# Three gate projections by one level of Strassen's algorithm, moved behind the attention stages

## The chip, the cores and the metric

The kernel runs on one core of a Trainium2 chip. The metric is the device time of one execution in microseconds (us); the time before is the median of three runs.

## The reference, cut to what matters

One encoder layer for 512 tokens of width 1024, all in float32. What the change touches are the three gates, the three branch outputs and their merge:

```python
u = rmsnorm(h, g_mix)                       # (512, 1024)
proj = u @ w_in                             # columns: GLA q,k,v,gg,alpha | FoX q,k,v,f | mq | 3 gates x 1024
y_gla = (rmsnorm(gla(...), g_gla_head) * silu(gg)) @ w_gla_o     # (512,512) @ (512,1024)
y_fox = forgetting_attention(...) @ w_fox_o
y_mem = memory_attention(...) @ w_mem_o
gt = sigmoid(gates.reshape(B, S, 3, D))     # gates = u @ the last 3 x 1024 columns of w_in
merged = gt[:, :, 0] * y_gla + gt[:, :, 1] * y_fox + gt[:, :, 2] * y_mem
h = h + merged @ w_out
u2 = rmsnorm(h, g_ffn)
h = h + square(relu(u2 @ w_ff1)) @ w_ff2
return rmsnorm(h, g_final)
```

## The kernel before, in words

Every large product is done as three matmuls (`mm3`, L151 to L153): both operands are split into a high part (a cast to the reduced format fp32r, on ScalarE, ACT) and a low part (the rest, by a subtraction on VectorE, DVE), and high by high, high by low and low by high are summed in PSUM. Weights come from HBM in chunks of 128 x 1024 (512 KB, by SyncE's queue, SP, into a ring of three `raw` tiles); `get_w` loads one and splits it into `hi` and `lo` tiles, rings of three each (L142, L143 for most; `split`, L201 and L202, elsewhere).

Two helpers use a chunk. `gT` keeps 128 output columns of the weight stationary and streams all 512 tokens (u is held transposed, channels on partitions, as `uhi` and `ulo`): 8 steps of 3 matmuls, and the result is transposed, channels by tokens. `gN` keeps 128 tokens stationary and streams 512 weight columns: the result has tokens on partitions. Both are generators: a *unit* is one step of three matmuls with 512 moving columns, and `weave` puts a given number of units of filler behind each step of an attention stage, so that TensorE (PE) has work while ACT and DVE do the softmax or the decays. The order of instructions on PE is the order written in the code. On the other engines a scheduler sets it when the program is built, and each engine, and the DMA queue of each, then works in that order.

The stages in order: the projections of memory and of u (front); FoX attention in 4 pairs of heads (`fox_scores`, `fox_turn`, `fox_values`), filled with projections; memory attention in 4 heads (`mem_scores`, `mem_turn`, `mem_values`), filled with `branch("gate_fox", ...)`; GLA (`decays`, `key_turn`, `gla_scores`, `states`, `gla_intra`, `gla_values`, `gla_turn`), filled with `branch("gate_mem", ...)`; then `branch("gate_gla", ...)` alone; then the product with `w_out`, the norm, and the MLP, both of whose products are already done by one level of Strassen's algorithm (7 block products in place of 8).

`branch` goes over 8 tiles of 128 channels: 24 matmuls for the gate, tanh on ACT (a sigmoid up to scale), 12 matmuls for the branch output, DVE multiplies both (L607), GpSimd (POOL) adds to `acc` (L608). The third branch also splits the sum into `mh` and `ml` (L611, L612), the stationary operands of `w_out`.

In the MLP's second product, `factor` makes sums of weight blocks by a DMA that adds in SBUF: SP loads a block into `b11` or `b12`, and POOL's queue (L1044) adds the next one onto it after the block before has been split. Sums of blocks of `w_ff1` (`T1` to `T4` for each quarter, 32 transfers in all) are made in HBM by POOL's queue beforehand (`next_sum`, L127 and L129), each released by the cast of some weight chunk.

Names in the order of instructions: `mm` and `a` are PSUM tiles (four banks each), `hi`/`lo`/`whi`/`wlo`/`flo` split weights, `th` the gate's tanh.

Of the kernel before, what the change touches and what calls it, by code (L numbers as in the profile page):

```python
# [9 lines left out]
F32 = mybir.dt.float32  # L10
# [7 lines left out]
P = 128  # L18
# [14 lines left out]
def chunk_list():  # L33
# [29 lines left out]
def hybrid_block(ctx, tc, chunks, wst, xT, memT, xN, cols, gffn, gfin, wup, cst, out):  # L63
# [140 lines left out]
    def sq_cols(pool_, src, n, k, accs, pool_ks, tag):  # L204
# [3 lines left out]
        if accs[e] is None:  # L208
            accs[e] = pool_.tile([P, n], F32, tag=f"{tag}_acc{e}", name=nm("acc"))
# [47 lines left out]
    sg = [gp.tile([P, S], F32, name=f"sg{j}") for j in range(4)]  # L257
    ofh = [ofp.tile([P, S], F32R, name=f"ofh{j}") for j in range(4)]
# [6 lines left out]
    with pool("front") as fp:  # L265
        rmb = gv[:, 0, 0:M]
        rxb = fp.tile([P, S], F32, name="rxb")
# [88 lines left out]
        for k in range(KT):  # L356
            ut = fp.tile([P, S], F32, tag="ut", name=nm("ut"), bufs=3)
# [216 lines left out]
    edge = mst.enter_context(pool("edge", side="right"))
    edge.tile([P, 112], F32, name="edge_pad")
    mp = mst.enter_context(pool("merge", side="right"))
    acc = [mp.tile([P, S], F32, name=f"acc{j}") for j in range(KT)]

    ogp = mst.enter_context(pool("ogla", side="right"))
    ogh = [ogp.tile([P, S], F32R, name=f"ogh{j}") for j in range(4)]  # L580
    ogl = [ogp.tile([P, S], F32R, name=f"ogl{j}") for j in range(4)]
    omst = ExitStack()
    omp = omst.enter_context(pool("omem", side="right"))
    omh = [omp.tile([P, S], F32R, name=f"omh{j}") for j in range(4)]
    oml = [omp.tile([P, S], F32R, name=f"oml{j}") for j in range(4)]

    def branch(gate, wo, oh, ol, n, last=None):
        cur = {}

        def gate_evac(ps):  # L590
            cur["th"] = th = mp.tile([P, S], F32, tag="th", name=nm("th"))
            nc.scalar.activation(th, ps, AF.Tanh, scale=0.5)

        for j in range(KT):
            yield from gT(("T", "w_in", OFF[gate] + P * j), uhi, ulo, gate_evac)
            th = cur["th"]
            if j % 2 == 0:
                ow = [t.rearrange("p (j k c) -> p j k c", j=2, k=4) for t in get_w(("O", wo, j // 2))]
            py = mmt()
            for k in range(4):  # L600
                mm3(py, ow[0][:, j % 2, k, :], ow[1][:, j % 2, k, :], oh[k], ol[k], k == 0, k == 3)
                if k < 3:
                    yield
            if n == 0:
                nc.vector.scalar_tensor_tensor(acc[j], th, 1.0, py, op0=ALU.add, op1=ALU.mult)
            else:
                nc.vector.scalar_tensor_tensor(th, th, 1.0, py, op0=ALU.add, op1=ALU.mult)  # L607
                nc.gpsimd.tensor_tensor(acc[j], acc[j], th, op=ALU.add)  # L608
            if last is not None:
                h, l = last  # L610
                nc.scalar.mul(h[:, j, :], acc[j], 0.5)  # L611
                nc.vector.scalar_tensor_tensor(l[:, j, :], acc[j], 0.5, f(h[:, j, :]), op0=ALU.mult, op1=ALU.subtract)  # L612
            yield


    with pool("mematt") as ap:
# [3 lines left out]
        def mem_q(h):  # L620
# [3 lines left out]
            return proj(OFF["mq"] + P * h, evac)  # L624
# [34 lines left out]
        def mem_values(h):  # L659
# [5 lines left out]
            split(omh[h], oml[h], po)  # L665
# [9 lines left out]
    ofst.close()  # L675


    with pool("gla") as lp:
        NC = 8
        half = [slice(64 * e, 64 * e + 64) for e in range(2)]  # L680
        gs = {}

        def decays(j):
            pb = at_()
            for t in range(NT):
                nc.tensor.matmul(pb[:, t * P:(t + 1) * P], la[:, t, j * P:(j + 1) * P], tri64, start=True, stop=True)
            ep, en, ek, kn, kp = (lp.tile([P, S], F32, name=f"{n}{j}") for n in ("ep", "en", "ek", "kn", "kp"))
            bl = small(lp, NC, f"bl{j}").rearrange("p (c o) -> p c o", o=1)
            dec = small(lp, NC, f"dec{j}")
            ek3, pb3 = (x.rearrange("p (c t) -> p c t", c=NC) for x in (ek, pb))  # L690
            nc.vector.tensor_copy(bl, pb3[:, :, 63:64])
            nc.vector.tensor_tensor(ek3, pb3, bl.to_broadcast([P, NC, 64]), op=ALU.subtract)
            nc.scalar.activation(ep, pb, AF.Exp)
            nc.scalar.activation(en, pb, AF.Exp, scale=-1.0)
            nc.scalar.activation(ek, ek, AF.Exp, scale=-1.0)
# [544 lines left out]
```

## Time and profile before

| | |
|---|---|
| runs | 831.17, 831.18, 829.07 us; median 831.17 us |
| profiled execution | 831.07 us, of which the traced span is 829.3 us |
| granted TensorE clock, mean | 0.992 |
| busy, share of the span | PE 98%, PE weight load 84%, DVE 63%, ACT 50%, POOL 14% |
| moved | 148.15 MB, mean 179 GB/s |

The profile has times in microseconds from the start of the span and one line for an instruction or a group of them (the line in the code, the engine, the operation, the tile written, an arrow, the tiles read, the shape, a count). Matmuls overlap, so that what one costs is the distance between two starts, not its listed duration. The three stages of attention lie at 91 to 208 us (FoX), 208 to 310 us (memory) and 310 to 381 us (GLA); the third branch ends at 454.5 us, the norm behind `w_out` at about 513 us, the MLP at about 820 us.

### The profile page before, as it was taken

To read this page: it belongs to the slowest core of one execution; us is meant where nothing else is said; L and a number is where in the kernel's file an instruction comes from. 1 tells how busy PE (TensorE), PEld (TensorE's weight loads), DVE (VectorE), ACT (ScalarE), POOL (GpSimd) and SP (SyncE) were. 2 spreads that over 40 slices of the span, in tenths; PEclk is the share of its full clock that TensorE was granted. 3 is DMA by queue.
4 is the path that set the end of the run, shared out by engine and by line. 5 is a ranking of instruction groups with operands and counts; after the bars stand their busy time and mean duration, and the time that the engine had idled before them with its cause. 6 is when DMAs were issued, how large, how long until landed. Compare 5 with 4: busy or idle time off the path is not lost.

```text
span 829.3 us, 11999 instructions
## 1 busy us (share of the span) xinstructions
PE 812.4 (98%) x4665; PEld 693.0 (84%) x4665; DVE 521.5 (63%) x799; ACT 417.5 (50%) x672; POOL 116.4 (14%) x124
## 2 busy tenths in 40 slices
PE   8999999999999999999999999999999999999994
PEld 5888787787888888888888889988998899889983
DVE  5783535554344546556434458895788778878886
ACT  7673544453233434233323336775676367547764
POOL 5211211000000001242122100011001100100122
PEclk9999999999999999999999999999999999999998
DMA  8445654335554637359676624878758966895674
GB/s 312 146 153 179 174 163 142 107 128 143 162 137 163 183 133 197 120 181 308 182 224 178 204 77 136 273 166 222 234 169 198 217 215 166 193 261 192 142 139 127
DMA packets 37577, 148.15 MB, mean 179 GB/s; under 512 B 4568, under 2 KB 5648, under 8 KB 35472
## 3 DMA queue, kind: packets, MB, share of 16 engines
q1 hardware_dynamic: 27648, 94.93, 32.7%
q0 software_dynamic: 8032, 47.71, 27.1%
q10 hardware_dynamic: 1840, 4.75, 1.7%
q8 instruction: 36, 0.59, 0.3%
q14 instruction: 21, 0.17, 0.1%
HBM read 143.68 MB, written 31.49 MB: 211 GB/s over the span
## 4 chain that ended last, share of the span: by engine, by line
PE 95%; DVE 2%; DMA 1%; issue 1%; ACT 0%; SPq 0%; POOLq 0%; POOL 0%; DVEq 0%
PE mm L151 27%; PE mm L153 26%; PE mm L152 26%; PE a L152 3%; PE a L151 3%; PE a L153 3%; PE a L479 1%; PE a L517 1%; DMA cst_s<-in_cst_dram 1%; DMA memr<-in_memT_dram 1%; PE a L503 0%; PE a L656 0%; PE a L855 0%; DVE h L908 0%; PE a L506 0%
## 5 line engine op out<-in xcount | busy, mean ns | idle before, releaser
L143 DVE TENSOR_TENSOR wlo<-raw,whi 128x1024 fp32r<-128x1024 f32 x75 | 97.3, 1300 | 112.7 <-ACT whi L142 111.9
L142 ACT CAST whi<-raw 128x1024 fp32r<-128x1024 f32 x75 | 78.6, 1051 | 138.9 <-PE mm L152 100.7
L151 PE MATMUL mm<-uhi,whi 128*128 128x512 f32 x352 | 139.4, 396 | 0.0
L152 PE MATMUL mm<-ulo,whi 128*128 128x512 f32 x352 | 137.3, 390 | 0.0
L153 PE MATMUL mm<-uhi,wlo 128*128 128x512 f32 x352 | 137.1, 389 | 0.0
L201 ACT CAST hi<-raw 128x1024 fp32r<-128x1024 f32 x65 | 68.2, 1050 | 47.5 <-PE mm L152 34.4
L202 DVE TENSOR_TENSOR lo<-raw,hi 128x1024 fp32r<-128x1024 f32 x65 | 79.5, 1223 | 18.6 <-ACT hi L201 18.6
L151 PEld LDWEIGHTS mm<-uhi,whi 128*128 128x128 f32 x352 | 66.1, 188 | 15.2 <-issue 1.8
L153 PEld LDWEIGHTS mm<-uhi,wlo 128*128 128x128 f32 x352 | 66.1, 188 | 14.1
L152 PEld LDWEIGHTS mm<-ulo,whi 128*128 128x128 f32 x352 | 66.2, 188 | 12.9
L1044 POOL DMA_DIRECT2D b<-in_wst_dram x32 | 27.6, 864 | 264.1 <-DVE lo L202 203.0
L153 PE MATMUL mm<-u2h,lo 128*128 128x256 f32 x224 | 63.4, 283 | 0.0
L152 PE MATMUL mm<-u2l,hi 128*128 128x256 f32 x224 | 63.4, 283 | 0.0
L151 PE MATMUL mm<-u2h,hi 128*128 128x256 f32 x224 | 63.4, 283 | 0.0
L151 PE MATMUL mm<-hi,ch 128*128 128x512 f32 x160 | 62.2, 389 | 0.0
L152 PE MATMUL mm<-lo,ch 128*128 128x512 f32 x160 | 62.2, 389 | 0.0
L153 PE MATMUL mm<-hi,cl 128*128 128x512 f32 x160 | 62.2, 389 | 0.0
L201 ACT CAST hi<-b 128x1024 fp32r<-128x1024 f32 x40 | 41.9, 1049 | 38.0 <-PE mm L153 27.2
L202 DVE TENSOR_TENSOR lo<-b,hi 128x1024 fp32r<-128x1024 f32 x40 | 48.9, 1223 | 18.0 <-ACT hi L201 17.7
L151 PE MATMUL mm<-u2sh,hi 128*128 128x256 f32 x168 | 47.5, 283 | 0.0
L152 PE MATMUL mm<-u2sl,hi 128*128 128x256 f32 x168 | 47.5, 283 | 0.0
L153 PE MATMUL mm<-u2sh,lo 128*128 128x256 f32 x168 | 47.5, 283 | 0.0
(334 smaller groups left out, 1810.6 us busy)
## 6 DMA issues: line engine op xcount, KB each, us to landing
raw<-in_wst_dram SPq DMA_DIRECT2D x121, 512.0 KB, 4.8
b<-in_wst_dram POOLq DMA_DIRECT2D x32, 512.0 KB, 5.4
raw<-T SPq DMA_DIRECT2D x28, 512.0 KB, 3.8
T<-in_wst_dram POOLq DMA_DIRECT2D x12, 1024.0 KB, 8.5
b<-in_wst_dram SPq DMA_DIRECT2D x16, 512.0 KB, 6.9
nFb<-dF ACTq DMA_DIRECT2D x8, 448.0 KB, 8.7
T<-in_wst_dram POOLq DMA_DIRECT2D x6, 512.0 KB, 5.9
xr<-in_xT_dram SPq DMA_DIRECT2D x4, 512.0 KB, 5.8
```

The costliest lines, as they stand in the source:

```text
L142: cast = nc.scalar.copy(hi, raw)
L143: nc.vector.tensor_tensor(lo, raw, f(hi), op=ALU.subtract)
L151: nc.tensor.matmul(ps, lh, rh, start=start, stop=False)
L152: nc.tensor.matmul(ps, lh, rl, start=False, stop=False)
L153: nc.tensor.matmul(ps, ll, rh, start=False, stop=stop)
L201: nc.scalar.copy(hi, src)
L202: return nc.vector.tensor_tensor(lo, src, f(hi), op=ALU.subtract).ins
L479: nc.tensor.matmul(pss[e][:, :w], q[half[e], sl], k[half[e], :w], start=a == 0, stop=a == 2)
L517: nc.tensor.matmul(po[half[e], kt * P:], V[:, kt, 2 * j + e, :], PT[e][:, c0:c0 + S - kt * P], start=kt == 0, stop=kt == 3, skip_group_che ...
L1044: nc.gpsimd.dma_start(to, x, accum_op=ALU.add)
```

## The change

The gates leave the attention stages. What fills those now is the rest: `gla_g` (the GLA out-gate, formerly in the FoX stage) and the three branch outputs (`y_out`), which come out in token order (`Y`, `YM`, `YG`) and are copied from PSUM by ACT. Behind attention stands a stage `gates`: each gate is a (512 x 1024) by (1024 x 1024) product, done as 7 block products with blocks of u stationary (256 tokens by 512 channels) and blocks of the weights streaming. Four sums of blocks of u are made once (`u_sum`). The weight sums are made as in the MLP: `fresh` loads a block into `B11` or `B12` by SP, and POOL's queue adds another onto it (L848) once it has been split. The sums of products are formed at evacuation (`gate_evac`), then tanh, times the branch output, added into `Y` (on POOL in the second gate, on DVE in the third). At the end PE transposes `Y` in 8 groups of four (`turn`) into the stationary operands of `w_out`.

```diff
     def next_sum(after):
         chunk_n[0] += 1
-        op = next(sums, None) if chunk_n[0] > 8 and chunk_n[0] % 2 else None
+        op = next(sums, None) if chunk_n[0] > 6 and chunk_n[0] % 3 else None
...
         for j in range(4):                     # FoX stage
-            steps += [(6, partial(scores, j, 0)), (8, partial(scores, j, 2))]
-            steps += [(9, *([partial(fox_values, j - 1)] if j else []), partial(fox_turn, 0)), (9, partial(fox_turn, 1))]
+            steps += [(5, partial(scores, j, 0)), (6, partial(scores, j, 2))]
+            steps += [(7, *([partial(fox_values, j - 1)] if j else []), partial(fox_turn, 0)), (6, partial(fox_turn, 1))]
...
+    def y_out(wo, lhs, to):
+        for c in range(2):
+            yield from gN([("N", wo, 2 * j, 512 * c) for j in range(2)], lhs, NT, mmt,
+                          lambda t, ps, c=c: nc.scalar.copy(to[:, t, 512 * c:512 * c + 512], ps))
...
         for h in range(6):                     # memory stage
-            for fn, i in ((mem_values, h - 2), (mem_turn, h - 1), (lambda i: run(mem_q(i)), h + 1), (mem_scores, h)):
+            for units, fn, i in ((3, mem_values, h - 2), (3 if h < 4 else 6, mem_turn, h - 1),
+                                 (1, lambda i: run(mem_q(i)), h + 1), (5, mem_scores, h)):
                 if 0 <= i < 4:
-                    steps.append(partial(fn, i))
-        weave([(6, st) for st in steps], branch("gate_fox", "w_fox_o", ofh, ofl, 0))
+                    steps.append((units, partial(fn, i)))
+            if h == 2:
+                steps.append((0, partial(decays, (dct, dcs), 0)))
+        weave(steps, gla_g(ap, 0), gla_g(ap, 1), y_out("w_fox_o", ..., Y))
...
-        steps = [call(20, decays, 0, 1), call(0, key_turn, 0), call(8, gla_scores, 0), call(0, key_turn, 1), call(8, gla_scores, 1),
-                 call(12, states, 0, 1), call(4, gla_intra, 0, 1), call(22, gla_values, 0, 1), call(0, gla_turn, *range(4))]
-        weave(steps, branch("gate_mem", "w_mem_o", omh, oml, 1))
+        steps = [(4, partial(decays, (dct1, dcs1), 1)), call(0, key_turn, 0), call(6, gla_scores, 0), call(0, key_turn, 1),
+                 call(6, gla_scores, 1), call(8, states, 0, 1), call(4, gla_intra, 0, 1), call(14, gla_values, 0, 1),
+                 call(6, gla_turn, *range(4))]
+        weave(steps, gla_g(lp, 2), gla_g(lp, 3), y_out("w_mem_o", ..., YM))
...
+    with pool("gates") as tp:
+        def fresh(g, b, to):
+            for i in range(2):
+                nc.sync.dma_start(to[i], block(g, b, i))
+        def factor(g, n, i):
+            if n in (2, 3):
+                raw = wp.tile([P, 1024], F32, tag="raw", name=nm("raw"))
+                nc.sync.dma_start(raw, block(g, {2: "21", 3: "22"}[n], i))
+                return halves(raw, n == 2)
+            to, x = {1: (B11, None), 7: (B12, "22"), 5: (B11, "12"), 6: (B12, "11"), 4: (B12, "21")}[n]
+            if x is not None:
+                nc.gpsimd.dma_start(to[i], block(g, x, i), accum_op=ALU.add)
+            return halves(to[i])
+        def gating(g, t, c, th):
+            nc.scalar.activation(th, th, AF.Tanh, scale=0.5)
+            y, to = (x[:, t, 512 * c:512 * c + 512] for x in (ys[g], Y))
+            if g == 0:
+                nc.vector.scalar_tensor_tensor(to, th, 1.0, y, op0=ALU.add, op1=ALU.mult)
+            else:
+                nc.vector.scalar_tensor_tensor(th, th, 1.0, y, op0=ALU.add, op1=ALU.mult)
+                (nc.vector if g == 2 else nc.gpsimd).tensor_tensor(to, to, th, op=ALU.add)
+        def gate_evac(g, n, t, ps):
+            if n == 1:
+                nc.scalar.copy(X[t], ps)
...
+            if n == 6:
+                nc.vector.tensor_tensor(X[t], X[t], ps, op=ALU.subtract)
+                nc.vector.tensor_tensor(G[t], held[5][t], X[t], op=ALU.subtract)
+                nc.vector.tensor_tensor(th, G[t], held[7][t], op=ALU.subtract)
+                gating(g, 2 + t, 1, th)
+            if n == 3:
+                nc.vector.tensor_tensor(th, G[t], ps, op=ALU.add)
+                gating(g, t, 1, th)
+            if n == 4:
+                nc.vector.tensor_tensor(th, X[t], ps, op=ALU.add)
+                gating(g, 2 + t, 0, th)
+        def gate(g):
+            for n in (1, 2, 7, 5, 6, 3, 4):
+                lh, ll = lhs_of(n)
+                for i in range(2):
+                    wh, wl = factor(g, n, i)
+                    if i == 1 and g < 2 and n in (5, 4):
+                        fresh(g + 1, *{5: ("11", B11), 4: ("12", B12)}[n])
+                    for t in range(2):
+                        for kk in range(2):
+                            # three matmuls with 512 columns into ps[t]: one unit
...
+                            yield
+        def turn(t, c):
+            pt = at_([P, 4, P])
+            for k in range(4):
+                nc.tensor.transpose(pt[:, k, :], Y[:, t, (4 * c + k) * P:(4 * c + k + 1) * P], ident)
+            hi, lo = (x[:, 4 * c:4 * c + 4, t * P:t * P + P] for x in (og, ml))
+            nc.scalar.mul(hi, pt, 0.5)
+            nc.vector.scalar_tensor_tensor(lo, pt, 0.5, f(hi), op0=ALU.mult, op1=ALU.subtract)
+        weave([(8,), (8, partial(u_sum, 7)), (8, partial(u_sum, 5)), (6, partial(u_sum, 6)), (2, partial(u_sum, 3))],
+              y_out("w_gla_o", ..., YG))
+        run(first, gate(1))          # first = gate(0)
+        last = gate(2)
+        run(islice(last, 42)); turn(0, 0); run(islice(last, 2)); turn(1, 0)
+        run(islice(last, 6));  turn(2, 1); run(islice(last, 2)); turn(3, 1)
+        run(islice(last, 3));  turn(0, 1); run(last);            turn(1, 1)
...
-        run(branch("gate_gla", "w_gla_o", ogh, ogl, 2, last=(mh, ml)))
...
-        run(gN([("N", "w_out", 2 * j, 0) for j in range(4)], of(mh, ml), NT, at_, res_evac(0)))
+        banks = [mmt() for _ in range(NT)]
+        for j in (2, 3, 0, 1):       # w_out, first half of its columns; after 14 units: turn(2, 0), turn(3, 0)
...
```

How this moves instructions, at three places. The first is PE where the gates end and `w_out` begins. Before, the last rows of the third branch (`mm_583` is its eighth output tile) are followed at once by the first of `w_out`:

```order
L151 MATMUL mm_583_3934<-ogh3_1933,whi_575_3879 128x512
L152 MATMUL mm_583_3934<-ogl3_1937,whi_575_3879 128x512
L153 MATMUL mm_583_3934<-ogh3_1933,wlo_576_3880 128x512
L151 MATMUL a_584_3961<-whi_589_3967,mh_3515 128x512
L152 MATMUL a_584_3961<-wlo_590_3968,mh_3515 128x512
```

Now PE meets transposes of `Y` inside the third gate; these rows are the first half of its last product (n = 4, into `a_561` and `a_562`), with `turn(2, 1)` between them:

```order
L900 MATMUL a_561_3766<-hi_593_3951,uhi_94 128x512
L901 MATMUL a_561_3766<-lo_594_3952,uhi_94 128x512
L902 MATMUL a_561_3766<-hi_593_3951,ulo_95 128x512
L910 MATMUL a_595_3961<-cst_s_71,Y_1767 128x128 x4
L900 MATMUL a_562_3767<-hi_593_3951,uhi_94 128x512
L901 MATMUL a_562_3767<-lo_594_3952,uhi_94 128x512
L902 MATMUL a_562_3767<-hi_593_3951,ulo_95 128x512
```

PE's queue now holds a step that reads what DVE has written of this same gate. The second place is DVE's queue at the same point. Before, one multiplication by the branch output (L607) and one low part of the merged sum (L612) stand between two splits of weights (L143):

```order
L607 SCALAR_TENSOR_TENSOR th_567_3824<-th_567_3824,mm_568_3826 128x512
L143 TENSOR_TENSOR wlo_580_3903<-raw_578_3900,whi_579_3902 128x1024
L612 SCALAR_TENSOR_TENSOR ml_3516<-acc5_1924,mh_3515 128x512
L143 TENSOR_TENSOR wlo_590_3968<-raw_588_3965,whi_589_3967 128x1024
L607 SCALAR_TENSOR_TENSOR th_573_3875<-th_573_3875,mm_577_3883 128x512
L612 SCALAR_TENSOR_TENSOR ml_3516<-acc6_1925,mh_3515 128x512
```

Now, from the evacuation of product 6 (`mm_573` and `mm_574`) on, with two more rows of its evacuation and a split ahead of these:

```order
L873 TENSOR_TENSOR th_579_3868<-G0_2917,a_561_3766 128x512
L873 TENSOR_TENSOR th_580_3881<-G1_2918,a_562_3767 128x512
L913 SCALAR_TENSOR_TENSOR ml_3682<-a_586_3902,og_2374 128x4x128
L202 TENSOR_TENSOR lo_598_3983<-g121_2914,hi_597_3982 128x1024
L857 SCALAR_TENSOR_TENSOR th_579_3868<-th_579_3868,YG_2919 128x512
L876 TENSOR_TENSOR th_591_3934<-G0_2917,mm_581_3888 128x512
L913 SCALAR_TENSOR_TENSOR ml_3682<-a_587_3915,og_2374 128x4x128
L857 SCALAR_TENSOR_TENSOR th_580_3881<-th_580_3881,YG_2919 128x512
L858 TENSOR_TENSOR Y_1767<-Y_1767,th_579_3868 128x512
L142 TENSOR_TENSOR wlo_610_4049<-raw_608_4046,whi_609_4048 128x1024
```

The addition into `Y` that `turn(2, 1)` reads (L858 of `th_579`) stands behind the evacuation of the other half and part of the next product's. The third place is POOL's queue. Before, in the third branch, it holds additions (L608) and transfers for the sums of `w_ff1`:

```order
L608 TENSOR_TENSOR acc2_1921<-acc2_1921,th_543_3660 128x512
L127 DMA T3_3_89<-in_wst_dram 128x2048
L608 TENSOR_TENSOR acc3_1922<-acc3_1922,th_552_3717 128x512
L129 DMA T2_3_88<-T1_3_87 16x16384
L608 TENSOR_TENSOR acc4_1923<-acc4_1923,th_558_3767 128x512
```

Now, where the second gate passes into the third, additions into `Y` (L858) stand between the transfers that add onto `B12` (`g120`, `g121`) and `B11` (`g110`, `g111`):

```order
L848 DMA g120_2913<-in_wst_dram 128x1024
L858 TENSOR_TENSOR Y_1767<-Y_1767,th_529_3568 128x512
L858 TENSOR_TENSOR Y_1767<-Y_1767,th_530_3581 128x512
L848 DMA g121_2914<-in_wst_dram 128x1024
L848 DMA g110_2911<-in_wst_dram 128x1024
L858 TENSOR_TENSOR Y_1767<-Y_1767,th_539_3620 128x512
L848 DMA g111_2912<-in_wst_dram 128x1024
L858 TENSOR_TENSOR Y_1767<-Y_1767,th_540_3631 128x512
```

An addition there waits until the transfer ahead of it in the queue has been issued, and that one waits for `fresh`'s load to land.

More of the change, by code (lines that the diff above doesn't have):

```diff
@@ L165, in gN @@
     def gN(keys, lhs, nt, mk, evac, tail=1, get=None):
-        pss = [mk() for _ in range(nt)]
+        pss = [mk() if mk else None for _ in range(nt)]
         n = len(keys)
@@ L208, in sq_cols @@
         if accs[e] is None:
-            accs[e] = pool_.tile([P, n], F32, tag=f"{tag}_acc{e}", name=nm("acc"))
+            accs[e] = dct[:, e * S:e * S + S] if n == S else pool_.tile([P, n], F32, tag=f"{tag}_acc{e}", name=nm("acc"))
             nc.scalar.activation(accs[e], src[:, k, :], AF.Square)
@@ L370, in mem_split, with proj @@
                 split(mvh[:, t, :], mvl[:, t, :], gqT[t])
+    def proj(c, evac, mk=mmt):
+        return gT(("T", "w_in", c), uhi, ulo, evac, mk=mk)
     with pool("fox") as xp:
-        gaT = xp.tile([P, S], F32, tag="tt", name="gaT")
+        gaT = dct[:, 1056:1056 + S]
         def low_rank():
@@ L573, in hybrid_block @@
+    keep = ctx.enter_context(pool("keep", side="right"))
+    keep.tile([P, 112], F32, name="edge_pad")
+    Y = keep.tile([P, NT, D], F32, name="Y")
     mst = ExitStack()
[L574 to L613, printed above, removed]
@@ new lines, in hybrid_block, with decays @@
+    gs = {}
+    NC = 8
+    def decays(tiles, j):
+        big, small_ = tiles
+        ep, en, ek, kn, kp = (big[:, i * S:i * S + S] for i in range(5))
+        bl = small_[:, :NC].rearrange("p (c o) -> p c o", o=1)
+        dec = small_[:, LINE:LINE + NC]
+        pb = at_()
+        for t in range(NT):
+            nc.tensor.matmul(pb[:, t * P:(t + 1) * P], la[:, t, j * P:(j + 1) * P], tri64, start=True, stop=True)
+        ek3, pb3 = (x.rearrange("p (c t) -> p c t", c=NC) for x in (ek, pb))
+        nc.vector.tensor_copy(bl, pb3[:, :, 63:64])
+        nc.vector.tensor_tensor(ek3, pb3, bl.to_broadcast([P, NC, 64]), op=ALU.subtract)
+        nc.scalar.activation(ep, pb, AF.Exp)
+        nc.scalar.activation(en, pb, AF.Exp, scale=-1.0)
+        nc.scalar.activation(ek, ek, AF.Exp, scale=-1.0)
+        nc.scalar.activation(dec, bl.rearrange("p c o -> p (c o)"), AF.Exp)
+        for to, x, y in ((ek, gkT, ek), (kn, gkT, en), (kp, gkT, ep), (ep, gqT, ep), (en, gqT, en)):
+            nc.vector.tensor_tensor(to, x[j], y, op=ALU.mult)
+        gs["d", j] = dec, ek, ((kn, ep), (kp, en))
@@ L674, in hybrid_block @@
+            if h == 2:
+                steps.append((0, partial(decays, (dct, dcs), 0)))
+        fox_o = [(ofh[k], ofl[k]) for k in range(4)]
+        weave(steps, gla_g(ap, 0), gla_g(ap, 1), y_out("w_fox_o", lambda k, sl: tuple(x[:, sl] for x in fox_o[k]), Y))
     kvst.close()
     ofst.close()
+    ogp = mst.enter_context(pool("ogla", side="right"))
+    og = ogp.tile([P, KT, S], F32R, name="og")
+    ymp = mst.enter_context(pool("ymem", side="right"))
+    YM = ymp.tile([P, NT, D], F32, tag="ym", name="YM")
@@ L678, in hybrid_block @@
     with pool("gla") as lp:
-        NC = 8
         half = [slice(64 * e, 64 * e + 64) for e in range(2)]
[L681 to L695, printed above, removed]
-            nc.scalar.activation(dec, bl.rearrange("p c o -> p (c o)"), AF.Exp)
-            for to, x, y in ((ek, gkT, ek), (kn, gkT, en), (kp, gkT, ep), (ep, gqT, ep), (en, gqT, en)):
-                nc.vector.tensor_tensor(to, x[j], y, op=ALU.mult)
-            gs["d", j] = dec, ek, ((kn, ep), (kp, en))
@@ L701, in key_turn, with part @@
+        dct1 = lp.tile([P, 5 * S], F32, name="dct1")
+        dcs1 = lp.tile([P, 2 * LINE], F32, name="dcs1")
+        big = (dct, dct1)
+        def part(j, i):
+            return big[j][:, i * S:i * S + S]
         def key_turn(j):
@@ L844, in out_w @@
             return own_w(key) if key[2] < 4 else get_w(key)
-        run(gN([("N", "w_out", 2 * j, 0) for j in range(4)], of(mh, ml), NT, at_, res_evac(0)))
-        c1 = gN([("N", "w_out", 2 * j, 512) for j in range(4)], of(mh, ml), NT, mmt, res_evac(1), tail=4, get=out_w)
+        banks = [mmt() for _ in range(NT)]
+        n = 0
+        for j in (2, 3, 0, 1):
+            wh, wl = (x.rearrange("p (k c) -> p k c", k=2) for x in get_w(("N", "w_out", 2 * j, 0)))
+            for t in (2, 3, 0, 1) if j > 1 else range(NT):
+                for kk in range(2):
+                    k = 2 * j + kk
+                    sl = slice(t * P, t * P + P)
+                    mm3(banks[t], mh[:, k, sl], ml[:, k, sl], wh[:, kk, :], wl[:, kk, :], k == 4, k == 3)
+                    n += 1
+                    if n == 14:
+                        turn(2, 0)
+                        turn(3, 0)
+                if j == 1:
+                    res_evac(0)(t, banks[t])
+        c1 = gN([("N", "w_out", 2 * j, 512) for j in range(4)], of(mh, ml), NT, None, res_evac(1), tail=4, get=out_w)
         run(islice(c1, 24))
@@ L898, in hybrid_block @@
         NQ = 4
-        held = {}
+        held.clear()
+        assert next(sums, None) is None
         def scratch():
```

161 lines of the change are left out of this document (122 added, 39 removed).

## The prediction

> **What bounds the kernel now.** I read the busy times and the chain that ended last on the page, then the waits of PE, then windows by stage, then the timeline at the places that the change touches.
>
> ```profile
> PE 812.4 (98%) x4665; PEld 693.0 (84%) x4665; DVE 521.5 (63%) x799; ACT 417.5 (50%) x672; POOL 116.4 (14%) x124
> PE 95%; DVE 2%; DMA 1%; issue 1%; ACT 0%; SPq 0%; POOLq 0%; POOL 0%; DVEq 0%
> ```
>
> PE is busy for 98% of the span and the chain runs through it for 95%. The view of waits, for PE alone, has five rows in all:
>
> ```profile
> PE mm L153 <- DVE lo L282: 1.9, 4, 0.8
> PE a L292 <- POOL wz L289: 1.3, 1, 1.3
> PE a L238 <- ACT dg L237: 1.0, 1, 1.0
> PE mm L151 <- ACT hi L281: 0.8, 1, 0.8
> PE a L222 <- DVE acc L214: 0.2, 1, 0.2
> ```
>
> Together 5.2 us, on lines of the front stage, which the change leaves as they are. Everywhere else PE finds its operands ready. So a matmul removed is its full price gained, a transpose added is its full price lost, and the question is only whether PE begins to wait. By stage (FoX, memory, GLA, MLP):
>
> ```profile
> core 0: us, PE busy (x) PEld busy (x) DVE busy (x) ACT busy (x) POOL busy (x), PEclk, DMA share, GB/s
> 91.40:208.30 116.90, 116.90 (x626) 90.99 (x625) 60.45 (x168) 54.88 (x118) 10.45 (x12) 1.00 0.46 138
> 208.30:310.30 102.00, 102.00 (x490) 85.70 (x489) 45.41 (x77) 36.09 (x72) 5.34 (x8) 1.00 0.51 155
> 310.30:381.00 70.70, 70.70 (x605) 58.58 (x605) 45.62 (x84) 25.82 (x44) 16.70 (x15) 1.00 0.60 167
> 513.00:820.00 307.00, 304.68 (x1899) 276.17 (x1897) 250.96 (x310) 196.18 (x266) 34.51 (x40) 1.00 0.75 197
> ```
>
> The clock is whole. In the MLP, which works as the gates will, DVE is busy 251 of 307 us (82%) and PE still meets no wait.
>
> **Matmuls removed.** The price of one with 512 columns is a distance of starts in the first half of `w_out`:
>
> ```profile
> 454.53 0.39 PE L151 MATMUL a<-whi,mh 128*128 128x512 f32 x1
> 476.29 0.39 PE L151 MATMUL mm<-fhi,mh 128*128 128x512 f32 x1
> ```
>
> Between these lie 4 x 4 x 2 x 3 = 96 matmuls: 21.76/96 = 0.2267 us. The gates had 3 x 8 x 8 x 3 = 576; 7 block products of 8 units of 3 make 168 a gate, 504. The branch outputs, `gla_g` and the rest keep their number. 72 x 0.2267 = 16.3 us saved.
>
> **Transposes added.** 8 `turn`s of 4. The nearest row is 8 transposes (L855) between matmuls:
>
> ```profile
> 492.38 0.39 PE L153 MATMUL mm<-whi,ml 128*128 128x512 f32 x1
> 492.62 1.04 PE L855 MATMUL a<-cst_s,un 128*128 128x128 f32 x8
> 493.41 0.48 PE L151 MATMUL mm<-fhi,mh 128*128 128x512 f32 x1
> 493.72 0.40 PE L152 MATMUL mm<-flo,mh 128*128 128x512 f32 x1
> ```
>
> Eight take 0.79 us, 32 take 3.2. The first matmul behind takes 0.31 instead of 0.23; seven such breaks are 0.6. Sum +3.8 us. If every cover below holds, the profiled execution of 831.07 becomes 831.07 - 16.3 + 3.8 = 818.6 us. (It lies 0.1 below the median of the runs, 831.17, so the sum stands for the median.)
>
> **Evacuations and splits.** All below is priced by these rows:
>
> ```profile
> L202 DVE TENSOR_TENSOR lo<-b,hi 128x1024 fp32r<-128x1024 f32 x40 | 48.9, 1223 | 18.0 <-ACT hi L201 17.7
> L201 ACT CAST hi<-b 128x1024 fp32r<-128x1024 f32 x40 | 41.9, 1049 | 38.0 <-PE mm L153 27.2
> 92.62 1.22 DVE L143 TENSOR_TENSOR wlo<-raw,whi 128x1024 fp32r<-128x1024 f32 x1
> 93.75 0.42 DVE L491 CUSTOM_DVE_ANT_1 P<-a,nFb 128x256 f32<-128x256 f32 x1
> 315.88 0.69 DVE L698 TENSOR_TENSOR ek<-gkT,ek 128x512 f32<-128x512 f32 x1
> 316.48 0.69 DVE L698 TENSOR_TENSOR en<-gqT,en 128x512 f32<-128x512 f32 x1
> ```
>
> A split costs DVE 1.22 us listed (1.13 from start to start), a 512-wide step 0.69 (0.60). A gate is 168 x 0.2267 = 38.1 us of PE. It asks of DVE 14 splits (17.1) and 18 steps (six subtractions, four sums, eight multiplications: 12.4): 29.5 of 38.1, or 77%, less than the MLP's 82%. ACT has 14 casts (14.7) and 12 short steps: half. Covered in the first two gates. The third puts its 6 additions and 2 more on DVE, and the low parts of the turns: 38 to 42 of 38. There DVE runs late.
>
> The four sums of blocks of u cost DVE 6 to 8 steps of 1024 elements and 4 splits of that size, at 1.22 us each some 15, and with waits for POOL's two subtractions 16 to 20. They lie beside the third branch output, 32 units or 96 matmuls of PE (21.8 us), and the first of them is asked for only two products of the first gate later (10.9 us). I cost them at nothing; without that cover they would be on the path whole.
>
> The turns for product 6, `turn(2, 1)` and `turn(3, 1)`, stand 36 matmuls and two turns behind the end of that product's first half: 8.2 + 0.9 = 9.1 us. In DVE's queue until the addition they need stand the rest of a split (1.0), two splits (2 x 1.13) and twelve short steps (12 x 0.60): 10.5 us, so PE waits 1.4 (by listed durations 2.7). The turns after it (`turn(3, 1)`, `turn(1, 1)`) inherit about 0.5 and 1.5. I take +3.5 us; ends 0 (the steps overlap more) and 7 (listed durations throughout).
>
> **Additions on POOL.** In gates one and two the additions into `Y` stand between accumulating transfers. The nearest rows, a POOL addition and a DVE split that start together, twice:
>
> ```profile
> 331.28 1.28 POOL L608 TENSOR_TENSOR acc<-acc,th 128x512 f32<-128x512 f32 x1 [7.93 <-DVE th L607]
> 331.30 2.34 DVE L143 TENSOR_TENSOR wlo<-raw,whi 128x1024 fp32r<-128x1024 f32 x1
> 351.56 2.38 POOL L608 TENSOR_TENSOR acc<-acc,th 128x512 f32<-128x512 f32 x1 [1.62 <-DVE th L607]
> 351.56 1.23 DVE L143 TENSOR_TENSOR wlo<-raw,whi 128x1024 fp32r<-128x1024 f32 x1
> ```
>
> Whichever starts second waits for the other: once the split takes 2.34 instead of 1.23 us, once the addition 2.38. [...] The second gate has 8 additions (16 on POOL fell to 8). DVE has 8 us spare there, and the splits run about 3.0 us ahead of PE (rings of three), so most is hidden; but two additions at the boundary to gate three wait behind accumulating transfers that wait for fresh loads, and hold `th` (ring of three), on which DVE's next evacuation waits. I take +1.0 us, ends 0 and 4.
>
> **Transfers.** 24 more loads of 512 KB (12.6 MB) in SP's and POOL's queues:
>
> ```profile
> b<-in_wst_dram POOLq DMA_DIRECT2D x32, 512.0 KB, 5.4
> T<-in_wst_dram POOLq DMA_DIRECT2D x12, 1024.0 KB, 8.5
> b<-in_wst_dram SPq DMA_DIRECT2D x16, 512.0 KB, 6.9
> L1044 POOL DMA_DIRECT2D b<-in_wst_dram x32 | 27.6, 864 | 264.1 <-DVE lo L202 203.0
> ```
>
> `B12` serves products 7, 6 and 4, two products (10.9 us) apart. Its chain is split 2.3, issue 0.86, landing 5.4; the split of the next takes 2.3 of what is left, and some 5 us are slack: hidden until a landing reaches 10.5. A fresh load (6.9) and the accumulation on it (0.9 + 5.4) land about 4 us before gate two or three needs them. I cost this at nothing; what would bring it out is the second rival below.
>
> **Less fill in attention.** The filler shrinks by the gates. Each stage's margin at its tightest step:
>
> ```profile
> 224.78 0.40 PE L151 MATMUL mm<-uhi,whi 128*128 128x512 f32 x1
> 228.03 1.14 DVE L648 TENSOR_SCALAR Pm<-Pm,ri 128x256 f32<-128x256 f32 x4
> 228.90 1.09 PE L656 MATMUL a<-cst_s,Pm 128*128 128x128 f32 x8
> 98.08 0.50 PE L151 MATMUL mm<-uhi,whi 128*128 128x512 f32 x1
> 100.64 0.49 DVE L497 TENSOR_SCALAR P<-P,ri 128x512 f32<-128x512 f32 x1
> 357.39 0.50 PE L151 MATMUL mm<-uhi,whi 128*128 128x512 f32 x1
> 364.88 1.12 DVE L765 TENSOR_SCALAR on<-a,rr 128x128 f32<-128x128 f32 x4
> ```
>
> Memory, first head: `Pm` is whole at 229.17; with 15 matmuls of fill for 18, PE arrives at 224.78 + 3.4 = 228.2. The transposes follow `Pm` tile by tile, so +0.5 us (ends 0 and 1.5); the later heads' order leaves longer fill. FoX: P is done at 101.13, with 6 units of fill behind the scores PE arrives at 98.08 + 18 x 0.2267 = 102.2, 1.0 to spare. GLA: `on` is done at 366.0, 8.6 us behind 357.39; the 14 units of fill that are left behind `gla_values` are 42 matmuls or 9.5 us. These two hold, barely. The steps of DVE and ACT that belonged to the gates there (tanh, the multiplication, the addition of `acc`) leave the same stages, which can only bring P, `Pm` and `on` earlier.
>
> **The sum.** 831.07 - 16.3 + 3.8 + 3.5 + 1.0 + 0.5 = 823.6 us. All upper ends give 831.1, all lower ends 818.6.
>
> **The rivals.**
> 1. *Every cover holds*: 818.6 us. For it: the MLP runs by the same scheme without a wait. Against: it has no turn that needs its own product's evacuation inside the same stage.
> 2. *The accumulating chains come late (slower)*. Place: `B12` from product to product. The sums of `w_ff1` (12 transfers of 1 MB, landing 8.5 us) share POOL's queue, and with their new pace lie in the gates. Behind one, a landing is 8.5 + 5.4 = 13.9 against the 10.5 allowed: 3.4 us a link. A gate has four such links (products 7, 5, 6 and 4), three gates 12; with 8 of them behind a sum it is 8 x 3.4 = 27: 831.07 - 16.3 + 3.8 + 27 = 846. It decides from a landing of 11.5 us: then 12 links x 1.0 equal the 12.5 won (16.3 - 3.8). Against: loads into `b` among the MLP's land in 5.4. [...]
> 3. *POOL's additions shut out DVE each time*: 8 x 1.11 (2.34 - 1.23) = 8.9 us in gate two, if the 3.0 us of lead is already eaten by the boundary: 823.6 + 8.9 - 1.0 = 831.5, no change. Against: of the two pairs shown, DVE paid in one, and PE waited for neither.
> 4. *Attention waits for lost fill*: the DVE and ACT steps of FoX and GLA come later than before by more than their margin of 1.0 us. At some 1.2 us for each of 8 turns it is 9: 832, no change. Against: DVE has fewer other steps there (45 to 60 of 71 to 117 us before, with the gate's steps in it).
>
> **How the numbers follow.** The forecast (waits between 820 and 829) 0.60; rival 1 0.20; rival 2 0.08; rivals 3 and 4 0.06 each. A difference of 0.3% (2.5 us, below which this kernel's measurement tells nothing) is passed by the first two: faster 0.80. Rivals 3 and 4 make same 0.12, rival 2 makes slower 0.08. The range runs from 817.5 (1 us below rival 1, if the breaks at the turns cost nothing) to 831.0 (the sum of the upper ends); outside lie rival 2 and most of 3 and 4, no more than 2 in 10.
>
> **What would show it.** PE has 72 fewer rows of 512 columns and 32 more transposes; its busy time falls by 12 to 13 us. PE's waits get new rows: transposes for `Y` (some 3.5 us, three rows), `hi` or `lo` of the second or third gate (1), transposes of `Pm` (0.5). Wrong if PE waits in the gates for `B12`'s splits (rival 2: loads into it land in over 10 us), if splits of 2.3 us are many in gate two (3), or if waits for P or `on` appear (4).

## The result and the profile after

The changed kernel takes 844.31 us (842.72 to 845.93), the kernel before beside it 830.27: a ratio of 1.017, 95% interval 1.0142 to 1.0199. It is slower by 14 us where 823.6 us had been forecast, outside the range. The profiled execution took 843.29 us, its span 841.5 against 829.3, so 12.2 us are to be found in the traces. The matmuls that were to go did go:

```profile
PE 807.4 (96%) x4625; PEld 684.0 (81%) x4625; DVE 581.9 (69%) x867; ACT 460.2 (55%) x730; POOL 130.3 (15%) x142
```

4665 rows of PE became 4625, 72 fewer and 32 more. Yet PE's busy time fell by 5.0 us only, and the waits of PE, five rows before, are now these (us in total, times, longest; two rows of 0.3 and 0.2 are left out):

```profile
PE mm L900 <- ACT hi L201: 6.5, 1, 6.5
PE a L910 <- DVE Y L858: 3.0, 3, 1.5
PE mm L150 <- DVE h L968: 3.0, 1, 3.0
PE mm L152 <- DVE lo L284: 2.0, 4, 0.8
PE mm L152 <- DVE wlo L142: 1.4, 1, 1.4
PE mm L901 <- DVE lo L202: 1.4, 3, 0.6
PE mm L900 <- ACT X L862: 1.4, 1, 1.4
PE a L294 <- POOL wz L291: 1.3, 1, 1.3
PE a L648 <- DVE Pm L640: 1.1, 1, 1.1
PE a L238 <- ACT dg L237: 1.0, 1, 1.0
PE mm L150 <- ACT hi L283: 0.6, 1, 0.6
```

With those two they add up to 23.2 us, 18.0 more than before. The largest is on PE's timeline at product 6 of the second gate:

```profile
387.81 0.39 PE L902 MATMUL a<-hi,ulo 128*128 128x512 f32 x1
394.67 0.79 PE L900 MATMUL mm<-hi,sh 128*128 128x512 f32 x1 [6.47 <-ACT hi L201]
396.52 0.63 PE L902 MATMUL mm<-hi,sl 128*128 128x512 f32 x1
398.65 0.62 PE L901 MATMUL mm<-lo,sh 128*128 128x512 f32 x1
```

Two things are to be seen. First, `hi` is a split of `B12`, whose cast on ACT waits for a transfer; the cast, and POOL's queue where the transfer was issued:

```profile
393.57 1.04 ACT L201 CAST hi<-g 128x1024 fp32r<-128x1024 f32 x1 [12.44 <-DMA g<-in_wst_dram]
364.84 2.63 POOL L848 DMA_DIRECT2D g<-in_wst_dram  x3 [1.87 <-DMA g<-in_wst_dram]
369.54 0.84 POOL L126 DMA_DIRECT2D T<-in_wst_dram  x1 [2.08 <-DVE lo L202]
371.88 0.82 POOL L126 DMA_DIRECT2D T<-in_wst_dram  x1 [1.50 <-DVE lo L202]
375.00 0.87 POOL L848 DMA_DIRECT2D g<-in_wst_dram  x1 [2.30 <-DVE lo L202]
377.24 0.86 POOL L848 DMA_DIRECT2D g<-in_wst_dram  x1 [1.37 <-DVE lo L202]
```

The two accumulations for product 6 (375.00 and 377.24) stand behind two sums of `w_ff1` of 1 MB each, which stand behind three accumulations. The longest time from issue to landing of any transfer that touches the gate's blocks between 360 and 400 us, and the median of the two sums:

```profile
DMA to landing us min/median/max: 5.4/7.0/19.0
T<-in_wst_dram POOLq DMA_DIRECT2D x2, 1024.0 KB, 15.9
```

19.0 us, where 5.4 had been assumed and 10.5 held to be harmless. Second, between 396.52 and 398.65 five matmuls take 2.13 us, 0.43 each and not 0.23. The windows of 1 us (the column behind POOL's is the granted clock) show why:

```profile
392.00:393.00 1.00, 0.00 (x0) 0.00 (x0) 0.00 (x0) 0.00 (x0) 0.00 (x0) 0.65 1.12 311
398.00:399.00 1.00, 1.00 (x3) 0.79 (x3) 1.00 (x2) 0.36 (x1) 0.04 (x1) 0.50 0.66 78
399.00:400.00 1.00, 1.00 (x5) 0.78 (x4) 0.80 (x1) 0.00 (x0) 0.82 (x1) 0.93 1.00 201
```

PE stops at 388.2; the clock falls to half at about 392.3 (a mean of 0.65 is 0.3 us at full and 0.7 us at half clock), and comes back at 399.1, 4.4 us after work resumed. The wait thus costs another 2 us in slow matmuls. The same happens behind the wait for `h`:

```profile
487.63 0.61 PE L150 MATMUL mm<-fhi,og 128*128 128x512 f32 x1 [2.95 <-DVE h L968]
491.02 0.52 PE L152 MATMUL mm<-fhi,ml 128*128 128x512 f32 x1
```

Eight matmuls in 3.39 us, 1.6 more than at full clock. What a turn costs is seen from the matmuls around it; here `turn(0, 0)` and, between the last two rows, `turn(1, 0)`:

```profile
445.43 0.39 PE L902 MATMUL mm<-hi,sl 128*128 128x512 f32 x1
445.94 0.66 PE L910 MATMUL a<-cst_s,Y 128*128 128x128 f32 x4
446.35 0.48 PE L900 MATMUL mm<-hi,sh 128*128 128x512 f32 x1
446.67 0.39 PE L901 MATMUL mm<-lo,sh 128*128 128x512 f32 x1
447.59 0.40 PE L902 MATMUL mm<-hi,sl 128*128 128x512 f32 x1
448.50 0.39 PE L901 MATMUL mm<-lo,sh 128*128 128x512 f32 x1
```

From 445.43 to 446.67 are 1.24 us, of which two matmuls are 0.45: 0.79 for the first turn, the dearest. The second costs 0.91 - 0.45 = 0.46. By the same reckoning, with the listed waits taken out, the other four single turns cost 0.63, 0.64, 0.46 and 0.64, and the pair under `w_out` 0.90: 4.5 in all. The sum: -16.3 + 4.5 + 18.0 + 3.6 (half clock) = 9.8 of the 12.2. The last 2.4 us were not itemised; a part of them is short breaks beside the waits (around the wait of 1.42 us for `X` PE loses another 0.28).

### The profile page after: what moved, and what is told of

Read it like the earlier page. It is cut to its first block, busy times and chain, and to the rows that moved or that the text cites. A ratio compares the mean times of both kernels' runs of the same rounds, so it can differ in the third digit from the quotient of the medians.

```text
span 841.5 us, 12103 instructions
## 1 busy us (share of the span) xinstructions
PE 807.4 (96%) x4625; PEld 684.0 (81%) x4625; DVE 581.9 (69%) x867; ACT 460.2 (55%) x730; POOL 130.3 (15%) x142
## 3 DMA queue, kind: packets, MB, share of 16 engines
q0 software_dynamic: 11488, 60.30, 34.8%
## 5 line engine op out<-in xcount | busy, mean ns | idle before, releaser
L142 DVE TENSOR_TENSOR wlo<-raw,whi 128x1024 fp32r<-128x1024 f32 x51 | 64.5, 1268 | 84.6 <-ACT whi L141 84.6
L1202 POOL DMA_DIRECT2D Y<-in_wst_dram x32 | 27.4, 857 | 262.9 <-DVE lo L202 193.8
L201 ACT CAST hi<-Y 128x1024 fp32r<-128x1024 f32 x40 | 41.9, 1048 | 39.9 <-PE mm L152 29.4
L202 DVE TENSOR_TENSOR lo<-Y,hi 128x1024 fp32r<-128x1024 f32 x40 | 48.9, 1222 | 19.8 <-ACT hi L201 19.7
L202 DVE TENSOR_TENSOR lo<-g,hi 128x1024 fp32r<-128x1024 f32 x30 | 41.8, 1393 | 28.7 <-ACT hi L201 28.6
L201 ACT CAST hi<-g 128x1024 fp32r<-128x1024 f32 x30 | 31.6, 1053 | 38.8 <-DMA g<-in_wst_dram 18.0
L152 PE MATMUL mm<-uhi,wlo 128*128 128x512 f32 x128 | 50.1, 391 | 1.4 <-DVE wlo L142 1.4
L150 PE MATMUL mm<-uhi,whi 128*128 128x512 f32 x128 | 51.5, 402 | 0.0
L151 PE MATMUL mm<-ulo,whi 128*128 128x512 f32 x128 | 49.9, 390 | 0.0
L151 PEld LDWEIGHTS mm<-u2l,hi 128*128 128x128 f32 x224 | 43.0, 192 | 0.2
```

What stands on the lines that cost most here:

```text
L142: nc.vector.tensor_tensor(lo, raw, f(hi), op=ALU.subtract)
L150: nc.tensor.matmul(ps, lh, rh, start=start, stop=False)
L151: nc.tensor.matmul(ps, lh, rl, start=False, stop=False)
L152: nc.tensor.matmul(ps, ll, rh, start=False, stop=stop)
L201: nc.scalar.copy(hi, src)
L202: return nc.vector.tensor_tensor(lo, src, f(hi), op=ALU.subtract).ins
```

## The experiments

The theory after these traces: the gates lose to the order of transfers in POOL's queue, `w_out` to a bank that is evacuated late, the end of the third gate to DVE. The chief rival to the first is that the DMA engines are simply full there. The diffs show the lines that matter; the comments in them are added here.

**Sums one link later.** In the changed kernel the sums of `w_ff1` are released by product 2; here by product 3:

```diff
-                return halves(raw, n == 2)
+                return halves(raw, n == 3)
```

> The two 1 MB transfers for sums of w_ff1 that stood in POOL's queue ahead of product 6's accumulation in the second gate now stand behind product 4's; the same transfers, the same bytes. Theory (order in the queue): the accumulations for product 6 land in 6 to 10 us instead of some 18, PE's wait of 6.5 us for hi goes, with it the 0.5 us for lo and the slow matmuls behind it (2.2 us): 844.3 - 9 = 835 us. Rival (volume: the DMA engines are 0.9 busy there, whatever the order): the wait stays over 4 us, or comes back at another link, 842 to 845 us.

Measured: 838.4 us, ratio 1.0098 (1.0077 to 1.012). Product 6 no longer waits at all, with the same bytes in the same gate. Between 360 and 400 us the longest landing into the gate's blocks is 11.6 us, though the DMA engines are 0.98 busy there (0.94 in the changed kernel). But waits came back at the next links, where the third gate begins (and the one for `h` is 3.5 us, 0.5 longer):

```profile
PE mm L900 <- ACT X L862: 2.7, 1, 2.7
PE a L901 <- DVE lo L202: 2.3, 2, 1.5
PE a L900 <- ACT hi L201: 1.1, 1, 1.1
```

So the order decides which link is hit; the gain was 6 us, not 9. It was both: the theory was right on product 6, the rival on "comes back at another link".

**Sums in the third gate.** Product 2 releases none in the second gate, and both in the third:

```diff
-                return halves(raw, n == 2)
+                return halves(raw, n == 2 and g != 1, g == 2)     # third argument: release in any case
```

> The same two 1 MB transfers are put at the same place of the third gate instead of the second. Theory (order in the queue): no wait over 1 us at product 6 of the second gate, and a wait of 4 to 7 us for hi at product 6 of the third; total 841 to 845 us. Rival (volume): the second gate keeps a wait of 3 us or more, since 2 MB of some 14 left it, and the third gets 1 to 3; total 843 to 847 us.

Measured: 833.71 us, ratio 1.0045 (1.003 to 1.0061). POOL's queue in the third gate, and PE at its product 6:

```profile
411.79 0.84 POOL L126 DMA_DIRECT2D T<-in_wst_dram  x1
415.31 0.82 POOL L126 DMA_DIRECT2D T<-in_wst_dram  x1 [1.39 <-DVE lo L202]
417.86 0.86 POOL L848 DMA_DIRECT2D g<-in_wst_dram  x1
419.29 0.85 POOL L848 DMA_DIRECT2D g<-in_wst_dram  x1 [0.57 <-DVE lo L202]
432.03 0.50 PE L900 MATMUL mm<-hi,sh 128*128 128x512 f32 x1 [2.57 <-ACT hi L201]
```

The second gate's wait is gone, and one stands at product 6 of the third, as the order theory has it. It is 2.6 and not 4 to 7 us: the longest landing there (400 to 440 us) is 14.0 us, not 19.0, and why was not taken apart. The time fell further than the 841 to 845 us expected, in part because the wait for `h` was gone too; the transfers under `w_out` also moved, and which of them did it was not taken apart.

**A bank from the other ring.** `w_out`'s first half holds all four banks of the ring `mm` (it had the other ring before the change). Its first evacuation in DVE's queue:

```profile
484.49 2.49 DVE L142 TENSOR_TENSOR wlo<-raw,whi 128x1024 fp32r<-128x1024 f32 x2 [10.54 <-ACT whi L141]
486.90 1.28 DVE L968 TENSOR_TENSOR h<-h,mm 128x512 f32<-128x512 f32 x2
```

DVE stands idle for 10.5 us in front of two splits that cannot run yet, with the evacuation behind them; the second half's first matmul needs that bank.

```diff
-        banks = [mmt() for _ in range(NT)]
+        banks = [mmt() if t else at_() for t in range(NT)]
```

> One of the four PSUM banks of w_out's first half comes from the other ring, so that the second half finds a free bank. Theory (the second half waits for a bank whose evacuation stands in DVE's queue behind two splits that wait for PE): PE's wait of 3.0 us for h goes, and the slow matmuls behind it (1.8 us): 844.3 - 4.8 = 839.5 us. Rival (DVE is late as such): PE waits as long at the second tile or at the first chunk that DVE splits there, 843 to 845 us.

Measured: 838.36 us, ratio 1.0101 (1.0079 to 1.0122). The wait for `h` is gone, although DVE evacuates hardly earlier (486.20 for 486.90):

```profile
486.20 0.68 DVE L968 TENSOR_TENSOR h<-h,a 128x512 f32<-128x512 f32 x1
```

**Turns later.** Where `turn(2,1)`, `turn(3,1)`, `turn(0,1)` and `turn(1,1)` stand:

```diff
-        run(islice(last, 6)); turn(2, 1); run(islice(last, 2)); turn(3, 1); run(islice(last, 3)); turn(0, 1); run(last); turn(1, 1)
+        run(islice(last, 9)); turn(2, 1); run(islice(last, 2)); turn(3, 1); run(last)
+        ... in w_out's first chunk: turn(0, 1) behind its third unit, turn(1, 1) behind its sixth
```

> turn(2,1) and turn(3,1) come 3 units later, turn(0,1) and turn(1,1) go into w_out's first chunk. Theory (the turns only stand too early): the three waits for Y, 3.0 us together, go: 844.3 - 3 = 841 us. Rival (DVE is behind until 467 us, with no gap from 444 us on): waits of 2 to 4 us come back at the turns' new places or at w_out's first matmuls, for the low part ml: 843 to 845 us.

Measured: 839.83 us, ratio 1.0117 (1.0088 to 1.0145). The three waits for `Y` (3.0 us) became these, 2.8 us:

```profile
PE mm L152 <- DVE ml L913: 2.1, 3, 1.2
PE mm L150 <- ACT og L912: 0.7, 1, 0.7
```

The rival holds for the waits: the place of the turns moves the wait and does not remove it. What this kernel won stands elsewhere, at `h`, whose wait is not in its trace.

**All sums early, the base of what follows.** Every chunk of the attention stages releases a sum, so that none is left for the gates, and the bank is apart:

```diff
-        op = next(sums, None) if chunk_n[0] > 6 and chunk_n[0] % 3 else None
+        op = next(sums, None) if chunk_n[0] > 6 else None
-        banks = [mmt() for _ in range(NT)]
+        banks = [mmt() if t else at_() for t in range(NT)]
```

> All 32 transfers for sums of w_ff1 are issued during the attention stages (every chunk releases one, where it was two of three), so none stands in POOL's queue in the gates or under w_out; one bank of w_out's first half from the other ring, as in bank_apart. Theory (order in POOL's queue): no wait over 1.5 us for hi or lo in any gate, since every landing is below 10.5 us; 844.3 - 9.2 - 4.8 = 830 us, with Y (3.0), X (1.4), Pm (1.1) and wlo (1.4) left. Rival (the DMA engines are too full in the gates even so): a wait of 2 us or more stays at products 6 or 4, 833 to 838 us; or the attention stages now wait for raw loads.

Measured: 827.01 us, ratio 0.9965 (0.9951 to 0.9979): faster than before the change. No wait for `hi` is left in the gates and one of 0.5 for `lo`; attention waits no more than it did (1.1 us for `Pm`).

**Where the additions stand.** In the changed kernel the second gate's additions are POOL's. At its end the first of two accumulations onto a fresh block waits for that block, and additions stand behind it:

```profile
409.87 0.85 POOL L848 DMA_DIRECT2D g<-in_wst_dram  x1 [10.06 <-DMA g<-in_wst_dram]
410.44 2.84 POOL L858 TENSOR_TENSOR Y<-Y,th 128x512 f32<-128x512 f32 x2
```

Beside these two additions a split on DVE, 1.22 us at the median in the gates, takes 4.24, and the matmul that needs it starts as it ends:

```profile
410.13 4.24 DVE L202 TENSOR_TENSOR lo<-g,hi 128x1024 fp32r<-128x1024 f32 x1
414.43 0.50 PE L901 MATMUL mm<-lo,uhi 128*128 128x512 f32 x1 [0.40 <-DVE lo L202]
```

The next two kernels put, on the base, all additions on DVE, and all on POOL:

```diff
-                (nc.vector if g == 2 else nc.gpsimd).tensor_tensor(to, to, th, op=ALU.add)
+                nc.vector.tensor_tensor(to, to, th, op=ALU.add)      # early_dve;  nc.gpsimd in early_pool
```

> As early, and the second gate's 8 additions are done by DVE in place of POOL. Theory (at the boundary additions wait in POOL's queue behind transfers, hold th, and so DVE and X): the waits for X (1.4) and for lo near the boundary (about 1) go, 2 to 3 us less than early. Rival (DVE has no room for 8 x 0.6 = 4.8 us more): the splits come late in the second gate, 0 to 3 us more than early.

Measured: 824.21 us, ratio 0.9926 (0.9903 to 0.9949), 2.8 us below the base. The waits for `X` (1.4) and `lo` (0.5) are gone; DVE's 4.8 us more of work (8 x 0.6) show nowhere on PE, and where the second gate passes into the third (391 to 416 us) no split takes over 1.23 us.

> As early, and the third gate's 8 additions are done by POOL in place of DVE. Theory (DVE's backlog makes the turns wait): DVE has 4.8 us less in the third gate, the waits for Y fall from 3.0 to 1 us or less, 2 us less than early. Rival (an addition on POOL takes 1.3 to 2.4 us and shuts DVE out): the waits for Y stay or grow, 0 to 3 us more than early.

Measured: 828.26 us, ratio 0.998 (0.9966 to 0.9994). The rival: the waits at the turns are as long, and now POOL's:

```profile
PE a L910 <- POOL Y L858: 3.2, 2, 2.4
```

**Turns later, on the base.**

> As early, and the turns as in turns_later. Theory (both together): waits for Y of 3.0 us go, waits for ml of about 2 come, 1 us less than early. If the gates' end is DVE's backlog and nothing else, the time is that of early within 0.5 us.

Measured: 828.48 us, ratio 0.9984 (0.997 to 0.9998): no gain on the base's 0.9965. The waits for `Y` are gone, and 2.9 us for `ml` and `og` stand in their place.

**DVE's order at the turns.** On early_dve, the casts of `w_out`'s first two chunks are made to wait for additions into `Y`, so that their splits stand behind these in DVE's queue:

```diff
+            tc.add_manual_dep(cast.ins, behind.name, ...)     # behind: the addition of product 3, t = 0 and t = 1
```

> As early_dve, and the first two splits of w_out's weights are released only by the additions into Y of product 3 in the third gate, so that they stand behind them in DVE's queue (two splits of 1.2 us fewer ahead of the last turns). Theory (the turns wait for DVE's order, not for its whole work): the waits for Y fall from 2.95 us (1.15, 0.32, 1.48) to about 1.2, and w_out's first matmuls wait under 1 us: 1 to 2 us less than early_dve's 824.2. Rival (DVE's backlog is the bound): what the turns win, w_out's first matmuls lose, 824 to 825 us.

Measured: 822.74 us, ratio 0.9909 (0.9892 to 0.9926). Of three waits for `Y` one is left, and `w_out` waits for nothing. So it was not DVE's whole work: splits that were wanted some 8 us later stood ahead of additions that were wanted at once. The times alone (822.7 and 824.2, intervals that overlap) would not show it; the rows do.

**One unit of fill moved in memory attention.** On adds_first, one unit goes from behind the first `mem_turn` to behind the first head's scores:

```diff
-            (3 if h < 4 else 6, mem_turn, h - 1), ... (5, mem_scores, h)
+            (2 if h == 1 else 3 if h < 4 else 6, mem_turn, h - 1), ... (6 if h == 0 else 5, mem_scores, h)
```

> As adds_first, and one unit of fill more behind the first head's scores in the memory stage (one fewer behind mem_turn). Theory (this wait is lost fill): the wait of 1.14 us for Pm goes, the time is about 1 us below adds_first. Rival (the DVE step comes later by as much): the wait stays at 1 us.

Measured: 821.8 us, ratio 0.990 (0.9886 to 0.9915), the fastest of all. What is left of PE's waits beyond those that stood there before the change:

```profile
PE mm L155 <- DVE wlo L145: 1.5, 1, 1.5
PE a L915 <- DVE Y L863: 1.1, 1, 1.1
PE a L651 <- DVE Pm L643: 0.5, 1, 0.5
PE mm L153 <- ACT V L527: 0.3, 1, 0.3
```

The wait for `Pm` fell by 0.7 us; the time by 0.9, which the intervals do not tell from nothing.

**A wait filled.** On the changed kernel, matmuls whose result is overwritten stand where PE waits:

```diff
+                    if g == 1 and n == 6 and i == 0:
+                        for _ in range(24):
+                            nc.tensor.matmul(ps[0], uhi[:, 0, :P], uhi[:, 0, :], start=True, stop=True)
```

> The changed kernel with 24 matmuls of 512 columns (5.4 us) written ahead of product 6 of the second gate, into its own bank and then overwritten, in the place of the wait of 6.5 us. Theory (a wait of PE of some 2.5 us or more makes the granted clock fall to half for some 4 us): the wait left is 1 to 2 us, the granted clock stays at 1.00 behind it, and the 2.2 us of slow matmuls go: 844.3 - 2 = 842 us. Rival (the matmuls behind the wait are slow for another reason, such as the late transfers): they stay slow, 844 us or more.

Measured: 843.09 us, ratio 1.0163 (1.0143 to 1.0184), not told apart from the changed kernel's 1.017. The wait left was 2.6 us and one of 0.8 behind it, and the clock fell all the same, only later, at about 395.8 us (windows of 1 us):

```profile
394.00:395.00 1.00, 0.30 (x1) 0.30 (x2) 0.65 (x1) 0.22 (x1) 0.05 (x1) 1.00 0.02 4
396.00:397.00 1.00, 1.00 (x4) 0.80 (x3) 1.00 (x1) 0.78 (x1) 0.00 (x0) 0.50 0.56 49
```

The expected saving failed. That the slow matmuls are the clock's doing stands, since its column says 0.50 in this trace too; that 5.4 us of filler would keep it up does not.

## Why the prediction was wrong

**The matmuls** were right: 72 fewer. With the waits gone (all_fixed) PE is busy for 800.2 us against 812.4, 12.2 less where 12.5 was forecast. A part of that agreement is luck: 1.3 us lie in the front stage (84.8 us of PE up to 91.5 us against 86.1), which all_fixed's profiled execution ran at full clock and the one before at a mean of 0.96. From FoX on it is 10.9 us.

**The transfers, costed at nothing, are the step that failed.** With the half clock behind it this wait is 9.0 of the 20.7 us between forecast and result. The 5.4 us of landing was a median of the MLP's loads, and the sums were looked at only under a rival. Nor do its terms give the landing of 10.5 us that it held to be harmless: 2.3, 0.86, 5.4 and 2.3 fill the 10.9 us between products and leave no 5 us of slack. The bound was near all the same: the first accumulation, issued at 375.00, lets the cast start at 393.57, 18.6 us later, and PE waits 6.5, so some 12 us could be borne. The place of that rival was right (accumulations behind 1 MB sums in POOL's queue), and its 846 us lies near the 844.3; but its price was not: it counted 8 links late by 3.4 us, and one pair of links was late, with 6.5 + 0.5 us of waiting and 2 of half clock. The total agreed because other terms, below, filled it up. The order of POOL's queue in the new program showed the two sums ahead of product 6's accumulations; what stands ahead in that queue was not added to the landing.

The page of the profile lists one queue of the kind `software_dynamic`, `q0`. It moved 60.30 MB where it moved 47.71 before, and the 12.6 MB between them match the 24 accumulations of 512 KB that POOL issues into the gates' blocks; the sums are POOL's transfers too, and no other queue of that kind is listed. Landings are 19.0 us behind the sums and 11.6 at most in the same window with the sums moved, though the DMA engines are about as full (0.94 from 360 to 400 us, 0.91 with the sums in the third gate and 0.98 with them one link later).

**`w_out`'s banks were overlooked.** The diff shows `banks = [mmt() ...]` where `at_` stood. The prediction took from it the turns only; it cost 3.0 us of waiting and 1.6 of half clock. Which instruction frees a bank, and what stands ahead of that one on its engine, was the question to ask.

**The half clock was not in the sum.** Every wait was priced at its length. Behind the two longest the clock took another 3.6 us.

**The turns** were near: 4.5 us for 3.8. The price came from eight transposes in a row; a group of four alone costs about half of that (0.46) in two places, 0.63 or 0.64 beside each of the three waits for `Y`, and 0.79 once.

**The end of the third gate** was right: 3.0 us in three waits (1.15, 0.34 and 1.51) for 3.5 forecast, on DVE's queue. **The boundary** came to 2.4 us of waits (`X` 1.4, `lo` 0.4 and 0.6) for 1.0 forecast, inside its ends of 0 and 4, but not by the mechanism that was priced. From 403.7 to 426 us DVE has no gap, so it did not stand waiting for `th`; it was slow. Additions held up behind the accumulation at 409.87 ran beside its splits, and these took 4.24, 2.45 and 1.91 us for 1.22, and a multiplication 1.77 for 0.68: 6.0 us more, beside 2.4 of waits on PE. So the rival that POOL shuts out DVE came in part, at the boundary and not each time: early_dve, which gives all of the second gate's additions to DVE, won 2.8 us and not 8.9. It takes away both the hold-up in POOL's queue and the shutting out; no run parts the two. **The lost fill** cost 1.1 us for 0.5, inside its ends; FoX and GLA held.

**Left open:** the wait of 1.4 us for `wlo` at 44 us, in the front stage that the prediction took for unchanged (tiles of it were renamed, and DVE's order there is another). No run tried it.

## What to carry to other kernels

Where an engine is busy 98% of the time, removing its work is the easy half of the estimate: list what each new wait hangs on, and for a transfer add up all that stands ahead of it in its own queue, not the median landing (here 19.0 us behind two sums of 1 MB, where 5.4 had been assumed). A change that moves many parts is tried with each wait taken away by itself; here four small edits (when the sums are issued, one bank, which engine adds, DVE's order) turned 1.4 to 2.0% slower into 1% faster. And an instruction that cannot run yet is best kept from standing in an engine's queue ahead of one that can: the wait of 3.0 us for `h` here was of that kind, with DVE idle for 10.5 us in front of two splits and the evacuation behind them.

## What the hardware showed

A wait of PE had a second price here. After waits of 6.5 and 3.0 us (the changed kernel) and of 2.6 us (keep_warm, with one of 0.8 close behind it) the granted clock fell to 0.50, not at once but 3 to 5 us after the wait began, and came back 3.4 us later, or 6.8; the matmuls that fell into that time took 0.43 us each for 0.23. In turns_later, after a wait of 7.6 us, it fell after 2.5 us and came back after 10.2. The length of the wait alone does not decide: in sums_after_link one of 2.7 us left the clock at 1.00, and behind three of 1.5, 1.1 and 0.8 us within 7 us it fell, while behind the three at the turns of the changed kernel (1.2, 0.3, 1.5) it did not. What decides beside the length was not shown.

A second fact is that of the boundary: beside two additions of POOL a DVE split of 1.22 us took 4.24, and with the additions on DVE (early_dve) none there took over 1.23.
